# One write and one read per token tile for the hidden activations' way through DRAM, and logits of two partition halves issued in turn, in a one-core encoder layer

## The chip, the core and the metric

The kernel runs on one core of one Trainium2 chip. A core has five engines with a queue of their own: TensorE (PE, with PEld for the loads of its stationary operand), VectorE (DVE), ScalarE (ACT), GpSimd (POOL) and SyncE (SP). POOL and SP issue the transfers (DMAs) that move data between DRAM and the on-chip memory; a queue is worked off in order, so an instruction that waits holds all that stand behind it. The metric is the device time of one execution in microseconds (us), as a median of several runs.

## The reference

One layer of a streaming encoder on 256 tokens of width 2048, in float32. Four residual blocks follow each other, each closed by a layer norm of `ALPHA * x + block(x)`:

```
x <- LN(alpha*x + 0.5*SwiGLU_1(x))                             D_FF = 5632
x <- LN(alpha*x + W_o[g_A*(DiffAttn(x) W_A) + g_B*(DSA(x) W_B)])
x <- LN(alpha*x + MemCrossAttn(x, mem))
x <- LN(alpha*x + 0.5*SwiGLU_2(x))

_swiglu(x) = (silu(x @ w_gate) * (x @ w_up)) @ w_down

DiffAttn: 8 heads, each with two softmaxes over keys of width 64,  p0 - lam * p1
DSA index: score = sum over 16 heads of width 64 of  relu(iq_h . ik) * iw_h ; the 64 best keys are kept
```

The two softmaxes of a DiffAttn head, and two index heads at a time, lie in one tile of 128 partitions: the first 64 partitions hold one half, the other 64 the other. These are the logits that the change speaks of. The other part of the change sits in both SwiGLUs, between the product with `w_up` and the product with `w_down`.

## The kernel before, in words

Every matrix product is made of three passes: both operands are split into a high and a low part (`whi`, `wlo` for weights, `hh`, `hl` for the hidden activations), and `mm3` (L174 to L176) issues high*high, high*low and low*high. ACT makes the high part (L170), DVE the low part (L171). Weights come in units of 128x1024 numbers, 512 KB each, loaded by SP into `raw` (L183). A unit feeds 12 matmuls of 512 columns, six for token tile t = 0 (tokens 0 to 127) and then six for t = 1. `Feed` loads and splits units ahead of their use, up to 10 in the first SwiGLU and 8 in the second. The order on each engine is the order of the code: generators ("tasks") are stepped once after each unit (`tasks.tick()`), and what a step issues stands in the queues at that place.

A SwiGLU takes its 11 column blocks of 512 in groups of 4, 4 and 3 (`FFN_GROUPS`). For each block it computes gate and up, and then a task turns h = silu(gate)*up, which lies with tokens on the partitions, into `hh` and `hl` with features on the partitions. After a group, the product with `w_down` runs over the group's blocks; its first quarter reaches the last block's `hh` after six units. For the last block of a SwiGLU TensorE does the turn (`h_task`). For the other ten blocks of each of the two SwiGLUs, twenty in all, the turn goes through DRAM (`h_bounced`): DVE multiplies (L503), one unit later it transposes 32x32 blocks within partitions (L506, from `hnat` into the old `silu` tile), POOL writes each of the two token tiles to DRAM (`h_dram`) with four transfers of 64 KB (L509) and reads it back in another arrangement with one of 256 KB (L512, into `hnat`), and five units later (`BOUNCE`) ACT and DVE make `hh` and `hl` out of what came back. POOL's queue holds all eight writes of a block first, then both reads; a read waits until the four writes of its token tile have landed.

Logits of width 64 are computed by `logits` for DiffAttn and by the same three-pass code in `index_task`. One call makes one half: 128 queries by 128 keys, then 128 queries by 256 keys (`SEG`), three passes each, six matmuls on one half of the partitions, into one PSUM tile `tp` (four buffers). The call for the other half follows at once, so a pair is 12 matmuls; there are eight pairs for DiffAttn and eight for the index.

Of the kernel before, what the change touches and what calls it, by code (L numbers as in the profile page):

```python
# [9 lines left out]
F32 = mybir.dt.float32  # L10
F32R = mybir.dt.float32r
AF = mybir.ActivationFunctionType
ALU = mybir.AluOpType
# [3 lines left out]
P = 128  # L17
# [4 lines left out]
NCOL = 512  # L22
# [11 lines left out]
SEG = ((0, 128), (128, 384))  # L34
# [116 lines left out]
def tile_encoder_layer(ctx, tc, a, out):  # L151
    nc = tc.nc
# [8 lines left out]
    dram = ctx.enter_context(tc.tile_pool(name="dram", bufs=1, space=bass.MemoryType.DRAM))  # L161
# [4 lines left out]
    def tp():  # L166
        return ps_tp.tile([P, NCOL], F32, name="tp")

    def split(hi, lo, src):
        nc.scalar.copy(hi, src)  # L170
        nc.vector.tensor_tensor(lo, src, hi.bitcast(F32), ALU.subtract)  # L171

    def mm3(dst, lh, ll, rh, rl, start, stop):
        nc.tensor.matmul(dst, lh, rh, start=start, stop=False)  # L174
        nc.tensor.matmul(dst, lh, rl, start=False, stop=False)  # L175
        nc.tensor.matmul(dst, ll, rh, start=False, stop=stop)  # L176
# [163 lines left out]
    def transposed(src, hi, lo, width=NCOL):  # L340

        p = blocks_T(src, width)[:, :width]
        split(hi, lo, p.rearrange("p (b t) -> p b t", t=P) if len(hi.shape) == 3 else p)

    def new_xT():
        return base.tile([P, 2, KD, T], F32R, name="xT")

# [136 lines left out]
    def ffn(pre, pool, y, xT, sts, lead, end):  # L484

        for gi, (c0, c1) in enumerate(FFN_GROUPS):
            hT = []

            def h_task(s, u, hh, hl):
                h = [pool.tile([P, NCOL], F32, name="hnat", bufs=3) for _ in range(2)]  # L490
                for t in range(2):
                    nc.vector.scalar_tensor_tensor(h[t], s[t], 0.5, u[t], op0=ALU.mult, op1=ALU.mult)
                yield
                for t in range(2):
                    sl = slice(t * P, (t + 1) * P)
                    transposed(h[t], hh[:, :, sl], hl[:, :, sl])

            def h_bounced(s, u, hh, hl):

                h = [pool.tile([P, NCOL], F32, name="hnat", bufs=3) for _ in range(2)]  # L500
                via = dram.tile([P, 2, 4, P], F32, name="h_dram", bufs=4)
                for t in range(2):
                    nc.vector.scalar_tensor_tensor(h[t], s[t], 0.5, u[t], op0=ALU.mult, op1=ALU.mult)  # L503
                yield
                for t in range(2):
                    nc.vector.transpose(s[t].rearrange("p (g b i) -> p g b i", b=4, i=32),  # L506
                                        h[t].rearrange("p (b g i) -> p g b i", b=4, i=32))
                    for q in range(4):
                        nc.gpsimd.dma_start(via[:, t, q].rearrange("(g i) c -> i g c", i=32),  # L509
                                            s[t][32 * q:32 * q + 32].rearrange("i (g c) -> i g c", g=4))  # L510
                for t in range(2):
                    nc.gpsimd.dma_start(h[t].rearrange("p (q c) -> p q c", q=4), via[:, t])  # L512
                for _ in range(BOUNCE):
                    yield
                for t in range(2):
                    sl = slice(t * P, (t + 1) * P)
                    split(hh[:, :, sl].rearrange("p b (q j) -> p b q j", j=32),
                          hl[:, :, sl].rearrange("p b (q j) -> p b q j", j=32),
                          h[t].rearrange("p (q b j) -> p b q j", b=4, j=32))

            for c in range(c0, c1):
                g = product(x_lhs(xT), pre + "_w_gate", c, dense(KD), lead=lead if c == 0 else 0)
                s = [pool.tile([P, NCOL], F32, name="silu", bufs=2) for _ in range(2)]
                for t in range(2):
                    nc.scalar.activation(s[t], g[t], AF.Silu)
                u = product(x_lhs(xT), pre + "_w_up", c, dense(KD))
                hh = pool.tile([P, 4, T], F32R, name="hh", bufs=4)
                hl = pool.tile([P, 4, T], F32R, name="hl", bufs=4)
                tasks.spawn((h_task if c == DFF // NCOL - 1 else h_bounced)(s, u, hh, hl))
                hT.append((hh, hl))  # L530

            def h_lhs(k, t):
                hh, hl = hT[k // 4]
                sl = slice(t * P, (t + 1) * P)
                return hh[:, k % 4, sl], hl[:, k % 4, sl]

            final = gi == len(FFN_GROUPS) - 1
            for n in range(4):
                kts = down_kts(c0, c1)
                if final and n == 3:  # L540
                    def after(t, d):
                        add_chunk(y, t, 3, d, 1.0, sts)
                        end(t)
                    product(h_lhs, pre + "_w_down", n, kts, trail=SKEW, after=after)
                else:
                    d = product(h_lhs, pre + "_w_down", n, kts)
                    for t in range(2):
                        add_chunk(y, t, n, d[t], 1.0 if gi else ALPHA, sts if final else None)
# [44 lines left out]
    with tc.tile_pool(name="att", bufs=1) as att:  # L593
# [34 lines left out]
        distm = att.tile([P, 384], F32, name="distm")  # L628
# [6 lines left out]
        score = att.tile([P, 384], F32, name="score")  # L635
# [17 lines left out]
        def logits(q, k, rowsl, blk):  # L653
            p = tp()
            for t, (s0, s1) in enumerate(SEG):
                ts_ = slice(t * P, (t + 1) * P)
                mm3(p[:, s0:s1], q[rowsl, 0, blk, ts_], q[rowsl, 1, blk, ts_],
                    k[rowsl, 0, blk, :s1 - s0], k[rowsl, 1, blk, :s1 - s0], True, True)
            return p

        def softmax_exp(dist, slope, p):

            e = att.tile([P, 384], F32, name="e", bufs=4)
            nc.vector.scalar_tensor_tensor(e, dist, -slope, p[:, :384], op0=ALU.mult, op1=ALU.add)
            nm = stat.tile([P, 2], F32, name="nm")
            sm = stat.tile([P, 2], F32, name="sm")
            for t, (s0, s1) in enumerate(SEG):
                nc.vector.tensor_reduce(nm[:, t:t + 1], e[:, s0:s1], AX.X, ALU.max, negate=True)  # L668
                nc.scalar.activation(e[:, s0:s1], e[:, s0:s1], AF.Exp, bias=nm[:, t:t + 1],  # L669
                                     accum_out=sm[:, t:t + 1])  # L670
            return e, sm
# [7 lines left out]

        def diff_head(q, k, v, b, g, r):  # L680
            slope = 2.0 ** -(4 * g + b + 1)
            es = []
            for c in range(2):
                es.append(softmax_exp(distm, slope, logits(q, k, slice(c * 64, c * 64 + 64), b)))
            yield
            (e0, s0), (e1, s1) = es
            r0 = stat.tile([P, 2], F32, name="r0")
# [4 lines left out]
            for t, (a0, a1) in enumerate(SEG):  # L692
                nc.scalar.mul(e1[:, a0:a1], e1[:, a0:a1], r1[:, t:t + 1])
                nc.vector.scalar_tensor_tensor(e0[:, a0:a1], e0[:, a0:a1], r0[:, t:t + 1], e1[:, a0:a1],
                                               op0=ALU.mult, op1=ALU.subtract)
# [48 lines left out]
        p = w_in(2)  # L744
# [42 lines left out]
        def index_task():  # L787
            while not (tik.done and tq1.done and d1.done):
                yield
            yield  # L790
            for h in range(16):
                iq, b, half = (iq0, iq1)[h // 8], h % 8 // 2, h % 2
                rowsl = slice(half * 64, half * 64 + 64)
                pl = tp()
                for t, (s0, s1) in enumerate(SEG):
                    ts_ = slice(t * P, (t + 1) * P)
                    mm3(pl[:, s0:s1], iq[rowsl, 0, b, ts_], iq[rowsl, 1, b, ts_],
                        ikT[rowsl, 0, :s1 - s0], ikT[rowsl, 1, :s1 - s0], True, True)
                r = att.tile([P, 384], F32, name="relu", bufs=2)
                nc.scalar.activation(r, pl[:, :384], AF.Relu)  # L800
                for t, (s0, s1) in enumerate(SEG):
                    nc.vector.scalar_tensor_tensor(score[:, s0:s1], r[:, s0:s1], iw[:, t, h:h + 1],
                                                   score[:, s0:s1], op0=ALU.mult, op1=ALU.add)
                if h % 2:
                    yield
            for i in range(TOPK // 8):
                for t, (s0, s1) in enumerate(SEG):
                    m8 = stat.tile([P, 8], F32, name="m8")
                    nc.vector.max(m8, score[:, s0:s1])
                    nc.vector.match_replace(score[:, s0:s1], m8, score[:, s0:s1], NEG)  # L810
                yield
            nc.vector.tensor_scalar(dists, score, -2e38, BIG, op0=ALU.is_gt, op1=ALU.mult)
            nc.vector.tensor_tensor(dists, dists, distm, ALU.add)
# [343 lines left out]
```

## Time and profile before

| what | value |
|---|---|
| median of 3 runs | 2259.43 us (2257.69 to 2259.87) |
| the profiled execution: its time, its span | 2260.71 us, 2258.9 us |
| PE, PEld busy | 2237.8 us (99%), 1850.0 us (82%) |
| DVE, ACT, POOL busy | 1308.0 us (58%), 1035.9 us (46%), 131.5 us (6%) |
| DMA: mean over the span | 203 GB/s; the weights' queue 62.2% of the 16 DMA engines' time, POOL's queue 3.4% |
| PE clock granted | over 0.9 in all forty slices |

The span is the stretch from the first to the last instruction that the profiler saw; the run's time is 1.8 us longer. Matmuls are pipelined, and the ends that the profile gives them are modelled, so that a row's duration is longer than the step to the next row: in the products a 128x512 matmul starts every 0.23 us and is shown as 0.39 us. For TensorE it is the starts that tell the cost. "From issue to landing" of a transfer counts from the start of its issue on the queue.

### The profile page before, as it was taken

The numbers are of one execution on the slowest core, as the hardware profiler recorded it, in microseconds if no ns is written. First come the engines' busy times: TensorE is split into PE (matmuls) and PEld (weight loads), VectorE is DVE, ScalarE is ACT, GpSimd is POOL, SyncE is SP. The second block draws the span as 40 slices with busy tenths as digits, with TensorE's granted clock in tenths as the row PEclk, the third lists the DMA queues.
The fourth block names the chain that finished last, engine by engine and source line by source line (L and its number), as shares of the span: only waits on it lengthen the run. The fifth ranks groups of instructions, "written<-read, shape, count | busy, mean of one in ns | idle before, by whom it ended". The sixth has DMA issues, their size and how long they took to land.

```text
span 2258.9 us, 27277 instructions
## 1 busy us (share of the span) xinstructions
PE 2237.8 (99%) x10248; PEld 1850.0 (82%) x10248; DVE 1308.0 (58%) x1498; ACT 1035.9 (46%) x1317; POOL 131.5 (6%) x236
## 2 busy tenths in 40 slices
PE   9999999999999999999999999999999999999997
PEld 7888888888888888888888888878888888888886
DVE  6555555554556666685655556777555455554554
ACT  5443344444443555655544444655444344434442
POOL 0100000100000000000000000000000001100100
PEclk9999999999999999999999999999999999999999
DMA  8877677766665655445567667557776666766762
GB/s 272 315 236 212 190 210 215 213 207 195 212 209 168 209 159 165 151 147 170 183 193 207 202 224 263 174 168 227 221 251 207 194 213 212 230 192 191 221 198 91
DMA packets 128916, 458.26 MB, mean 203 GB/s; under 512 B 16704, under 2 KB 16832, under 8 KB 127632
## 3 DMA queue, kind: packets, MB, share of 16 engines
q1 hardware_dynamic: 119520, 431.02, 62.2%
q0 software_dynamic: 9264, 25.51, 3.4%
q8 instruction: 80, 1.31, 0.2%
q14 instruction: 52, 0.43, 0.1%
HBM read 441.78 MB, written 14.68 MB: 202 GB/s over the span
## 4 chain that ended last, share of the span: by engine, by line
PE 94%; DMA 2%; issue 1%; DVE 1%; ACT 1%; POOL 0%; POOLq 0%; SPq 0%; DVEq 0%; ACTq 0%
PE acc L174 30%; PE acc L176 30%; PE acc L175 30%; PE tp L337 2%; DMA hnat<-h_dram 1%; DMA h_dram<-silu 1%; PE tp L174 1%; PE tp L175 1%; PE tp L176 0%; DMA raw<-in_ffn_w_gate 0%; ACT whi L170 0%; DVE wlo L171 0%; POOL h_dram L509 0%; DVE y L479 0%; ACT me L1010 0%
## 5 line engine op out<-in xcount | busy, mean ns | idle before, releaser
L171 DVE TENSOR_TENSOR wlo<-raw,whi 128x1024 fp32r<-128x1024 f32 (+1 forms) x787 | 958.3, 1222 | 811.3 <-ACT whi L170 808.7
L170 ACT CAST whi<-raw 128x1024 fp32r<-128x1024 f32 (+1 forms) x787 | 824.1, 1051 | 932.5 <-PE acc L176 874.2
L174 PE MATMUL acc<-whi,xT 128*128 128x512 f32 x2176 | 853.8, 392 | 1.7 <-ACT whi L170 1.7
L176 PE MATMUL acc<-whi,xT 128*128 128x512 f32 x2176 | 848.3, 390 | 0.0
L175 PE MATMUL acc<-wlo,xT 128*128 128x512 f32 x2176 | 848.2, 390 | 0.0
L174 PEld LDWEIGHTS acc<-whi,xT 128*128 128x128 f32 x2176 | 409.2, 188 | 87.1 <-ACT whi L170 3.3
L176 PEld LDWEIGHTS acc<-whi,xT 128*128 128x128 f32 x2176 | 409.0, 188 | 86.0
L175 PEld LDWEIGHTS acc<-wlo,xT 128*128 128x128 f32 x2176 | 409.4, 188 | 84.4 <-DVE wlo L171 0.9
L174 PE MATMUL acc<-whi,hh 128*128 128x512 f32 x704 | 274.9, 390 | 2.3 <-ACT hh L170 2.3
L176 PE MATMUL acc<-whi,hl 128*128 128x512 f32 x704 | 274.4, 390 | 0.0
L175 PE MATMUL acc<-wlo,hh 128*128 128x512 f32 x704 | 274.0, 389 | 0.0
L174 PEld LDWEIGHTS acc<-whi,hh 128*128 128x128 f32 x704 | 132.1, 188 | 30.9 <-ACT hh L170 4.0
L176 PEld LDWEIGHTS acc<-whi,hl 128*128 128x128 f32 x704 | 132.1, 188 | 29.1 <-DVE hl L171 1.7
L175 PEld LDWEIGHTS acc<-wlo,hh 128*128 128x128 f32 x704 | 132.2, 188 | 27.3
L509 POOL DMA_DIRECT2D h_dram<-silu x160 | 87.2, 553 | 1077.0 <-DVE silu L506 1027.2
L174 PE MATMUL acc<-whi,ring 128*128 128x512 f32 x144 | 56.7, 394 | 0.0
L176 PE MATMUL acc<-whi,ring 128*128 128x512 f32 x144 | 56.1, 390 | 0.0
L175 PE MATMUL acc<-wlo,ring 128*128 128x512 f32 x144 | 56.1, 389 | 0.0
L479 DVE SCALAR_TENSOR_TENSOR y<-y,acc 128x512 f32<-128x512 f32 x64 | 42.2, 679 | 17.3 <-PE acc L176 17.3
L669 ACT ACTIVATE e<-e,nm 128x128 f32<-128x128 f32 (+1 forms) x48 | 21.5, 448 | 45.7 <-DVE nm L668 44.8
L170 ACT CAST hh<-hnat 128x512 fp32r<-128x512 f32 x40 | 24.8, 621 | 37.7 <-DMA hnat<-h_dram 34.8
L171 DVE TENSOR_TENSOR hl<-hnat,hh 128x512 fp32r<-128x512 f32 x40 | 27.4, 691 | 25.2 <-ACT hh L170 25.2
(200 smaller groups left out, 1136.6 us busy)
## 6 DMA issues: line engine op xcount, KB each, us to landing
raw<-in_ffn_w_up SPq DMA_DIRECT2D x176, 512.0 KB, 4.4
raw<-in_ffn_w_down SPq DMA_DIRECT2D x176, 512.0 KB, 4.2
raw<-in_ffn_w_gate SPq DMA_DIRECT2D x175, 512.0 KB, 4.3
raw<-in_w_in SPq DMA_DIRECT2D x88, 512.0 KB, 3.6
raw<-in_w_gate SPq DMA_DIRECT2D x64, 512.0 KB, 4.1
raw<-in_w_mix_out SPq DMA_DIRECT2D x32, 512.0 KB, 4.4
h_dram<-silu POOLq DMA_DIRECT2D x160, 64.0 KB, 4.4
hnat<-h_dram POOLq DMA_DIRECT2D x40, 256.0 KB, 5.3
```

Source lines behind the costliest of these rows:

```text
L170: nc.scalar.copy(hi, src)
L171: nc.vector.tensor_tensor(lo, src, hi.bitcast(F32), ALU.subtract)
L174: nc.tensor.matmul(dst, lh, rh, start=start, stop=False)
L175: nc.tensor.matmul(dst, lh, rl, start=False, stop=False)
L176: nc.tensor.matmul(dst, ll, rh, start=False, stop=stop)
L337: nc.tensor.transpose(p[:, b * P:(b + 1) * P], src[:, b * P:(b + 1) * P], ident)
L479: nc.vector.scalar_tensor_tensor(c, c, scale, d, op0=ALU.mult, op1=ALU.add)
L509: nc.gpsimd.dma_start(via[:, t, q].rearrange("(g i) c -> i g c", i=32), s[t][32 * q:32 * q + 32].rearrange("i (g c) -> i g c", g=4))
L669: nc.scalar.activation(e[:, s0:s1], e[:, s0:s1], AF.Exp, bias=nm[:, t:t + 1], accum_out=sm[:, t:t + 1])
```

## The change

Two things are changed. First, in `h_bounced`, DVE transposes with another order of features in its input (`turn`: feature b*128 + i*4 + g instead of b*128 + g*32 + i), and a token tile is written by one transfer of 256 KB with rows of 2 KB and read back by one of 256 KB whose pieces are 512 bytes (`to_places`; before, the writes had pieces of 512 bytes and the read had rows of 2 KB). Both transfers of a token tile are issued before those of the other. The features end in the same places. Second, `twin_logits` computes both halves of a pair in one loop that goes to the other half after each matmul, into two PSUM tiles.

```diff
+    def turn(dst, src):
+        nc.vector.transpose(dst.rearrange("p (g b i) -> p b g i", b=4, i=32),
+                            src.rearrange("p (b i g) -> p b g i", b=4, i=32))
+
+    def to_places(dst, src):
+        via = dram.tile([P, NCOL], F32, name="via", bufs=6)
+        nc.gpsimd.dma_start(via, src)
+        nc.gpsimd.dma_start(dst.rearrange("p (q c) -> p q c", q=4),
+                            via.rearrange("(q i) (g c) -> (i g) q c", q=4, g=4))
...
             def h_bounced(s, u, hh, hl):
...
-                via = dram.tile([P, 2, 4, P], F32, name="h_dram", bufs=4)
...
                 for t in range(2):
-                    nc.vector.transpose(s[t].rearrange("p (g b i) -> p g b i", b=4, i=32),
-                                        h[t].rearrange("p (b g i) -> p g b i", b=4, i=32))
-                    for q in range(4):
-                        nc.gpsimd.dma_start(via[:, t, q].rearrange("(g i) c -> i g c", i=32),
-                                            s[t][32 * q:32 * q + 32].rearrange("i (g c) -> i g c", g=4))
-                for t in range(2):
-                    nc.gpsimd.dma_start(h[t].rearrange("p (q c) -> p q c", q=4), via[:, t])
+                    turn(s[t], h[t])
+                    to_places(h[t], s[t])
...
+        def twin_logits(q, blk, key):
+            p = [tp(), tp()]
+            for t, (s0, s1) in enumerate(SEG):
+                ts_ = slice(t * P, (t + 1) * P)
+                for i, (a, b) in enumerate(((0, 0), (0, 1), (1, 0))):
+                    for half in range(2):
+                        rowsl = slice(half * 64, half * 64 + 64)
+                        nc.tensor.matmul(p[half][:, s0:s1], q[rowsl, a, blk, ts_], key(rowsl, b, slice(s1 - s0)),
+                                         start=i == 0, stop=i == 2)
+            return p
...
-            es = []
-            for c in range(2):
-                es.append(softmax_exp(distm, slope, logits(q, k, slice(c * 64, c * 64 + 64), b)))
+            es = [softmax_exp(distm, slope, p) for p in twin_logits(q, b, lambda r, h, c: k[r, h, b, c])]
...
-            for h in range(16):
...
+            for h in range(0, 16, 2):
+                pls = twin_logits((iq0, iq1)[h // 8], h % 8 // 2, lambda r, i, c: ikT[r, i, c])
+                for half, pl in enumerate(pls):
...
```

On POOL, the first block of the first SwiGLU before (`silu_300` and `silu_301` are the two token tiles, `hnat_458` and `hnat_459` where they come back to; the waits on DMASW are waits for transfers of POOL's own to land):

```order
L509 DMA h_dram_460<-silu_300 32x4x128 [waits DVE_49,Activation_49]
L509 DMA h_dram_460<-silu_300 32x4x128 x3
L509 DMA h_dram_460<-silu_301 32x4x128 [waits DVE_49,Activation_49]
L509 DMA h_dram_460<-silu_301 32x4x128
L509 DMA h_dram_460<-silu_301 32x4x128 [waits DMASW0_49]
L509 DMA h_dram_460<-silu_301 32x4x128 [waits DMASW1_49]
L512 DMA hnat_458<-h_dram_460 128x512 [waits DMASW4_49,DMASW5_49,DMASW3_49,DMASW2_49]
L512 DMA hnat_459<-h_dram_460 128x512 [waits DMASW6_49,DMASW7_49,DMASW1_49,DMASW0_49]
```

The same place now, with the transfer ahead of it (of the constant `lnT`):

```order
L324 DMA lnT_80<-in_lnT 128x128
L354 DMA via_483<-silu_300 128x512 [waits DVE_49,Activation_49]
L355 DMA hnat_458<-via_483 128x4x128 [waits DMASW2_49]
L354 DMA via_487<-silu_301 128x512 [waits DVE_49,Activation_49]
L355 DMA hnat_459<-via_487 128x4x128 [waits DMASW4_49]
```

Ten rows became four, and the second token tile's write now stands behind the first token tile's read, which waits for the first write to land. On PE, the logits of the first DiffAttn pair before (`tp_5953` is the first half, `tp_5968` the second):

```order
L174 MATMUL tp_5953<-ring_5762,ring_5578 128x128
L175 MATMUL tp_5953<-ring_5762,ring_5578 128x128
L176 MATMUL tp_5953<-ring_5762,ring_5578 128x128
L174 MATMUL tp_5953<-ring_5762,ring_5578 128x256
L175 MATMUL tp_5953<-ring_5762,ring_5578 128x256
L176 MATMUL tp_5953<-ring_5762,ring_5578 128x256
L174 MATMUL tp_5968<-ring_5762,ring_5578 128x128
L175 MATMUL tp_5968<-ring_5762,ring_5578 128x128
L176 MATMUL tp_5968<-ring_5762,ring_5578 128x128
L174 MATMUL tp_5968<-ring_5762,ring_5578 128x256
L175 MATMUL tp_5968<-ring_5762,ring_5578 128x256
L176 MATMUL tp_5968<-ring_5762,ring_5578 128x256
```

The same place now (the two halves are `tp_5903` and `tp_5904`):

```order
L681 MATMUL tp_5903<-ring_5712,ring_5528 128x128
L681 MATMUL tp_5904<-ring_5712,ring_5528 128x128
L681 MATMUL tp_5903<-ring_5712,ring_5528 128x128
L681 MATMUL tp_5904<-ring_5712,ring_5528 128x128
L681 MATMUL tp_5903<-ring_5712,ring_5528 128x128
L681 MATMUL tp_5904<-ring_5712,ring_5528 128x128
L681 MATMUL tp_5903<-ring_5712,ring_5528 128x256
L681 MATMUL tp_5904<-ring_5712,ring_5528 128x256
L681 MATMUL tp_5903<-ring_5712,ring_5528 128x256
L681 MATMUL tp_5904<-ring_5712,ring_5528 128x256
L681 MATMUL tp_5903<-ring_5712,ring_5528 128x256
L681 MATMUL tp_5904<-ring_5712,ring_5528 128x256
```

The twelve matmuls are the same; the halves take turns. On DVE, ACT and SP the instructions stand in the order in which they stood before.

## Rows read from the trace of the kernel before

**Rows 1.** The page's first part: busy time and share of each engine.
```profile
PE 2237.8 (99%) x10248; PEld 1850.0 (82%) x10248; DVE 1308.0 (58%) x1498; ACT 1035.9 (46%) x1317; POOL 131.5 (6%) x236
```

**Rows 2.** The page's chain that ended last: shares by engine.
```profile
PE 94%; DMA 2%; issue 1%; DVE 1%; ACT 1%; POOL 0%; POOLq 0%; SPq 0%; DVEq 0%; ACTq 0%
```

**Rows 3.** Waits of PE, for hh: us in total, times, longest.
```profile
PE acc L174 <- ACT hh L170: 2.3, 4, 0.6
```

**Rows 4.** Waits of ACT, for PE: us in total, times, longest.
```profile
ACT whi L170 <- PE acc L176: 874.2, 536, 9.8
```

**Rows 5.** Timeline of weight loads in the first logit pair: start us, us, instruction.
```profile
805.08 0.18 PEld L174 LDWEIGHTS tp<-ring 64*128 64x128 f32 x1 [0.35 <-issue]
805.19 0.19 PEld L175 LDWEIGHTS tp<-ring 64*128 64x128 f32 x1
...
805.37 0.23 PEld L174 LDWEIGHTS tp<-ring 64*128 64x128 f32 x2
...
805.69 0.19 PEld L174 LDWEIGHTS tp<-ring 64*128 64x128 f32 x1
...
805.93 0.18 PEld L176 LDWEIGHTS tp<-ring 64*128 64x128 f32 x1
806.25 0.19 PEld L174 LDWEIGHTS acc<-whi,xT 128*128 128x128 f32 x1
```

**Rows 6.** The same timeline, a narrower stretch: the second of the merged two.
```profile
805.41 0.19 PEld L174 LDWEIGHTS tp<-ring 64*128 64x128 f32 x1
```

**Rows 7.** Timeline of matmuls around that pair.
```profile
804.76 0.39 PE L176 MATMUL acc<-whi,xT 128*128 128x512 f32 x1
...
806.25 0.50 PE L174 MATMUL acc<-whi,xT 128*128 128x512 f32 x1
806.59 0.39 PE L175 MATMUL acc<-wlo,xT 128*128 128x512 f32 x1
```

**Rows 8.** The chain at the first group's end: start us, us, what.
```profile
187.84 1.35 POOL h_dram L509 x3
...
189.49 4.77 DMA h_dram<-silu
...
194.33 0.51 issue
194.85 5.60 DMA hnat<-h_dram
```

**Rows 9.** Timeline of POOL there: the second token tile's read.
```profile
196.24 0.55 POOL L512 DMA_DIRECT2D hnat<-h_dram  x1 [0.84 <-DMA h_dram<-silu]
```

**Rows 10.** Timeline of ACT there: both casts of what came back.
```profile
200.53 0.62 ACT L170 CAST hh<-hnat 128x512 fp32r<-128x512 f32 x1 [1.54 <-DMA hnat<-h_dram]
201.65 0.62 ACT L170 CAST hh<-hnat 128x512 fp32r<-128x512 f32 x1 [0.50 <-DMA hnat<-h_dram]
```

**Rows 11.** Timeline of DVE there: the low part after a weight unit's.
```profile
199.02 1.23 DVE L171 TENSOR_TENSOR wlo<-raw,whi 128x1024 fp32r<-128x1024 f32 x1 [1.50 <-ACT whi L170]
201.18 0.69 DVE L171 TENSOR_TENSOR hl<-hnat,hh 128x512 fp32r<-128x512 f32 x1 [0.93 <-ACT hh L170]
```

**Rows 12.** Timeline of matmuls there: the last before the wait, the first and fourth behind.
```profile
200.23 0.39 PE L176 MATMUL acc<-whi,hl 128*128 128x512 f32 x1
201.20 0.50 PE L174 MATMUL acc<-whi,hh 128*128 128x512 f32 x1 [0.58 <-ACT hh L170]
...
202.26 0.40 PE L174 MATMUL acc<-whi,hh 128*128 128x512 f32 x1
```

**Rows 13.** The first 64 KB write of that block alone: issue, and time to landing.
```profile
L509 POOL DMA_DIRECT2D h_dram<-silu x1: 567/567/567, 187.8 to 187.8; - x1
...
DMA to landing us min/median/max: 3.4/3.4/3.4
```

**Rows 14.** The forty reads of L512, to landing.
```profile
DMA to landing us min/median/max: 3.7/5.3/6.3
```

**Rows 15.** DMA issues: writes of 256 KB from a 128x512 tile elsewhere; KB, median us to landing.
```profile
x_dram<-y POOLq DMA_DIRECT2D x8, 256.0 KB, 2.3
```

**Rows 16.** Those eight writes, to landing.
```profile
DMA to landing us min/median/max: 2.3/2.3/4.8
```

**Rows 17.** Costliest groups of DVE: the transposes.
```profile
L506 DVE STREAM_TRANSPOSE silu<-hnat 128x512 f32<-128x512 f32 x40 | 26.0, 687 | 0.0
```

More of the change, by code (lines that the diff above doesn't have):

```diff
@@ L343, in transposed, with in_order, groups @@
         split(hi, lo, p.rearrange("p (b t) -> p b t", t=P) if len(hi.shape) == 3 else p)
+    def turn(dst, src):
[6 more added lines that the diff above has]
+                            via.rearrange("(q i) (g c) -> (i g) q c", q=4, g=4))
+    def in_order(x):
+        return x.rearrange("p (q b j) -> p b q j", b=4, j=32)
+    def groups(x):
+        return x.rearrange("p b (q j) -> p b q j", j=32)
     def new_xT():
@@ L516, in h_bounced @@
                     sl = slice(t * P, (t + 1) * P)
-                    split(hh[:, :, sl].rearrange("p b (q j) -> p b q j", j=32),
-                          hl[:, :, sl].rearrange("p b (q j) -> p b q j", j=32),
-                          h[t].rearrange("p (q b j) -> p b q j", b=4, j=32))
+                    split(groups(hh[:, :, sl]), groups(hl[:, :, sl]), in_order(h[t]))
             for c in range(c0, c1):
@@ L790, in index_task @@
             yield
-            for h in range(16):
[L792 to L805, printed above, removed]
+            for h in range(0, 16, 2):
+                pls = twin_logits((iq0, iq1)[h // 8], h % 8 // 2, lambda r, i, c: ikT[r, i, c])
+                for half, pl in enumerate(pls):
+                    r = att.tile([P, 384], F32, name="relu", bufs=2)
+                    nc.scalar.activation(r, pl[:, :384], AF.Relu)
+                    for t, (s0, s1) in enumerate(SEG):
+                        nc.vector.scalar_tensor_tensor(score[:, s0:s1], r[:, s0:s1], iw[:, t, h + half:h + half + 1],
+                                                       score[:, s0:s1], op0=ALU.mult, op1=ALU.add)
+                yield
             for i in range(TOPK // 8):
```

## The prediction

> **What bounds the kernel now.** I read the page's busy times first, then its chain, then the waits of TensorE (PE), then the two stretches that the change touches. PE is busy for 99% of the span [rows 1], and 94% of the chain is PE [rows 2]. So a microsecond taken off PE's own steps is a microsecond off the end, and one on another engine counts only where PE waits for it. The splitting of weights is no limit: ACT spends 874 us waiting for PE to release a unit's place [rows 4], so PE always has units ready, some eight of them at 12 x 0.23 us each. Of the two SwiGLUs only one thing makes PE wait: four times it waits for `hh` [rows 3], at the end of the first and second group of each SwiGLU, where the last block of the group has come back from DRAM too late. The view counts 2.3 us, but the timeline shows more. The last matmul before the wait starts at 200.23; the next would start at 200.46, the fourth behind it at 201.14, and that fourth starts at 202.26 [rows 12]: 1.12 us are lost, 0.74 waiting for the high part and 0.38 after it, largely for the low part that DVE makes behind ACT. Four such places cost 4.5 us. At the other sixteen blocks a late `hh` makes only ACT and DVE wait, and the units in stock cover that.
>
> **Logits in turn: a gain of 3.7 us.** A pair of halves is 12 matmuls. Between the last product matmul before it, 804.76, and the second after it, 806.59 [rows 7], lie 1.83 us; two ordinary steps would take 0.46, so a pair costs 1.37 us, 16 pairs 22 us. How the time is spent is seen in the loads of the stationary operand. Within one half a load follows the one before by 0.11 us (805.08 to 805.19) [rows 5]. But where the second half has begun (805.37) while the first half's second segment (805.41 [rows 6]) is still running, loads of the two halves come 0.04 to 0.07 us apart, each half keeping its own 0.11 us. So the two halves of the partitions already work side by side, for the middle third: first three matmuls alone, then three and three together, then three alone, from 805.08 to 805.93 [rows 5], 0.85 us. Issued in turn, the two sides run together all the way: 11 steps of 0.055 us, and a little more for the 256-column ones, 0.62 us. Saved: 0.23 us a pair, 3.7 us in 16 pairs, all on PE. Upper bound: if both halves start together at each step, five steps of 0.11 to 0.12, 0.28 saved, 4.5 us. Lower bound: the pattern brings nothing (0), or a switch of halves after every matmul costs the full 0.11 us, 11 x 0.11 = 1.21 instead of 0.85, a loss of 5.8 us; the middle of the pair, where halves already alternate, speaks against that, and I don't count on it. The wait of the first half's softmax moves not at all or to earlier, since its last matmul now comes one step before the end of a shorter pair; ACT and DVE have room there.
>
> **The way through DRAM: a loss of 4 us at the four places, nothing elsewhere.** What is removed: POOL's issue of six of the eight writes of a block (8 x 0.55 us become 2 x 0.55). What is added: a wait in POOL's queue. Before, all eight writes were issued in a row and both reads followed; now the second token tile's write stands behind the first tile's read, and that read waits until the first write has landed. Two landings of writes stand in series where there was one.
>
> The old way at the first place: the first write is issued at 187.84, the last of the first tile lands at 194.33, its read is issued 0.52 us later and lands 5.60 us after that [rows 8]; the second tile's read is issued at 196.24 [rows 9] and has landed when ACT casts at 201.65 [rows 10], 13.8 us after the first issue. The new way, with W0 and W1 for the writes, R for the second read, 0.52 from a landing to the next issue and 0.56 for an issue of a read: W0 + 0.52 + 0.56 + W1 + 0.52 + R = W0 + W1 + R + 1.60.
>
> W has no row of its own kind. Elsewhere eight writes of the same size and shape took 2.3 us [rows 15], the slowest 4.8 [rows 16]; here, among the weights' transfers, the first 64 KB alone took 3.4 [rows 13], and a whole tile has four times that. I take W0 = 3.8, and W1 = 4.3, since it queues behind the first read. R: forty reads took 3.7 to 6.3, median 5.3 [rows 14]; the new read has pieces of 512 bytes instead of 2 KB, and I take 5.3. Sum: 15.0 us, so the second tile is there at 202.84 instead of 201.6, the first at about 197.5 instead of 200.45.
>
> Then at each of the four places: the first tile's high part is cast in time; its low part stands behind a weight unit's (199.02 + 1.23 [rows 11]), is ready at 200.97 and costs 0.1. The second tile is first needed six matmuls after 200.46, at 201.93 with that 0.1. Its high part is ready 0.70 us after landing (0.62 for the cast [rows 10] and the handing over), 203.54: 1.61 us of waiting, and 0.37 behind it as now. That makes 2.08 us instead of 1.12, a loss of 0.96, four times 3.8 us. From about 14.0 us on (landing at 201.9) the new way loses, with 4 us for each microsecond more.
>
> Bounds: with 2.3 + 2.3 + 3.7 + 1.6 = 9.9 us nothing is late but that 0.1, a gain of 4.1; with 4.8 + 4.8 + 6.3 + 1.6 = 17.5 the landing is at 205.34, 4.58 us a place, a loss of 13.8. DVE's transpose reads every fourth number now; at 687 ns for 512 columns [rows 17] it takes a number per column, and I leave it at that. Were it twice as long, the first write would start 0.69 later: 2.8 us in the four places, and the other 27 us hidden, as DVE is busy for 58% [rows 1].
>
> The Trainium skill, "DMA: Bandwidth & Descriptors", section "Anatomy of one DMA — SWDGE (gpsimd) path", fits a transfer as about 2.0 us plus its bytes at 436 GB/s. An estimate by it: 2.6 us for 256 KB, either way, so 9.4 us in all and the gain of 4.1 above. The quiet writes of [rows 15] agree; the 64 KB of [rows 13] took 3.4 where the fit gives 2.2, so among the weights it falls short.
>
> **Sum.** -3.7 + 3.8 = +0.1 us. The profiled execution took 2260.71 us, of which 2258.9 are the span, and lies 1.3 above the median of 2259.43; I set the difference against the median: 2259.5 us.
>
> **Rivals.**
> Quick writes (faster): the old writes were slow because of their 512-byte pieces, and rows of 2 KB land as in the quiet stretch, 2.3 to 3.4 us. For: [rows 15]. Against: 3.4 us for a mere 64 KB here [rows 13]. With 2.6 + 3.0 + 5.0 + 1.6 = 12.2 us the landing is at 200.0, before the need, and each place gains about 1.0: 4 us, with the logits 7.7, 2251.7 us. Decided by a landing before 13.8 us: from there on the sum is more than 4.5 us faster.
> Slow scattered reads (slower): a read of 512 pieces instead of 128 costs POOL or the transfer engines more. All POOL transfers in this trace have about 128 pieces and 0.55 us of issue, so whether issue goes by pieces isn't seen; if it did, each read would be issued in 2.2 us instead of 0.56, 1.65 later for the second write and 1.65 for the second read. 15.0 + 3.3 = 18.3 us, 5.4 us a place, 17 us lost: 2272.7 us. At 16.1 us, with slower reads and writes alone, the sum passes +4.5: 2264.
> The Trainium skill, "DMA: Bandwidth & Descriptors", in that same section, calls the making of descriptors small and says that many can be made before it shows; that speaks against the higher of these two prices, and no row here shows it either way.
> No gain from the logits: 2263.2 us, if the reordering that PE now does by itself leaves nothing to win.
>
> **How the numbers follow.** What a measurement of this kernel can tell from no change is about 0.2%, 4.5 us: 2254.9 to 2263.9. The forecast, a landing 13.8 to 16.1 us after the first issue with the logits' gain, 0.43, or without it, 0.03: within. Quick writes or a larger gain from the logits: 0.22, faster. Slow reads, serial writes over 16 us, a slower transpose: 0.32, slower. The likeliest alone spans 2255 to 2264; leaving out one in ten at each end, the range goes from the quick writes, 2252, to near the end of the slow ones, 2270.
>
> **What would show it.** In the changed kernel: loads of a pair 0.05 to 0.06 us apart from its first to its last, and 1.1 us for a pair instead of 1.37. On POOL: the second write issued a landing after the first, and the second read 9 to 11 us after the first write. On PE: the four waits for `hh` move from the first token tile's to the second's matmuls, about 2 us each. I am wrong if a write of 256 KB lands in under 3 us there (the waits vanish), if a read's issue on POOL takes far more than 0.56 us, or if the pair keeps its 0.85 us.

## The result: 0.6% slower, and the profile after

| | before | changed |
|---|---|---|
| median | 2258.59 us (6 runs) | 2272.18 us (6 runs, 2268.08 to 2276.19) |
| profiled execution: its time, its span | as in the table before | 2268.51 us, 2266.7 us |

The ratio is 1.0059, with a 95% interval of 1.0045 to 1.0073: slower by 13.6 us, and above the range of the prediction, which ended at 2270. The six runs of the changed kernel lie in two heaps, three near 2268.5 and three near 2275.7; the profiled execution belongs to the lower one, so it shows 9 to 10 us of the 13.6.

Busy times and the chain by engine, from the page of the changed kernel:

```profile
PE 2237.7 (99%) x10248; PEld 1848.3 (82%) x10248; DVE 1318.5 (58%) x1498; ACT 1029.0 (45%) x1317; POOL 74.0 (3%) x116
PE 93%; DMA 3%; issue 1%; DVE 1%; ACT 1%; POOL 0%; SPq 0%; POOLq 0%; ACTq 0%; DVEq 0%
```

PE's wait for `hh`, from its waits (us in total, times, longest):

```profile
PE acc L174 <- ACT hh L170: 10.3, 4, 4.6
```

POOL has 57.5 us less to do than in [rows 1], and the kernel is slower all the same. The wait of [rows 3] is still there at the same four places, but is 10.3 us instead of 2.3, and the longest is 4.6. The way of one block at the first place, from POOL's timeline (start us, us, instruction, idle before it and what ended it):

```profile
187.89 0.55 POOL L354 DMA_DIRECT2D via<-silu  x1 [30.86 <-ACT whi L170]
191.88 0.75 POOL L355 DMA_DIRECT2D hnat<-via  x1 [3.44 <-DVE wlo L171]
192.62 0.55 POOL L354 DMA_DIRECT2D via<-silu  x1
199.72 0.75 POOL L355 DMA_DIRECT2D hnat<-via  x1 [6.55 <-DMA via<-silu]
```

The wait before 191.88 is put down to DVE there; by its semaphore (under "The change") the read waits for the first write, which landed at 191.34. The chain of waits that ended last, in the same stretch:

```profile
187.89 3.45 DMA via<-silu
...
192.62 6.81 DMA via<-silu
199.43 0.28 issue
199.72 5.96 DMA hnat<-via
...
205.75 0.63 ACT hh L170
```

The first token tile's write needs 3.5 us, less than the four old writes; the second one's, of the same size and shape, 6.8. From the first issue to the second tile's landing it is 17.8 us (187.89 to 205.68), where it was at most 13.8 in [rows 8 to 10]. The first tile is in time now, but with its six matmuls done PE has nothing left to do. Matmuls there:

```profile
201.39 0.40 PE L176 MATMUL acc<-whi,hl 128*128 128x512 f32 x1
206.42 0.64 PE L174 MATMUL acc<-whi,hh 128*128 128x512 f32 x1 [4.63 <-ACT hh L170]
206.86 0.63 PE L175 MATMUL acc<-wlo,hh 128*128 128x512 f32 x1
207.29 0.65 PE L176 MATMUL acc<-whi,hl 128*128 128x512 f32 x1
...
209.45 0.63 PE L175 MATMUL acc<-wlo,hh 128*128 128x512 f32 x1
209.88 0.47 PE L176 MATMUL acc<-whi,hl 128*128 128x512 f32 x1
210.18 0.40 PE L174 MATMUL acc<-whi,hh 128*128 128x512 f32 x1
```

Two things are lost: a step of 5.03 us where 0.23 would do, and behind it eight steps of about 0.43 us instead of 0.23. The second is TensorE's clock. Windows of PE (length, busy time and count of each engine, granted clock, DMA share, GB/s) at the first, second and third place:

```profile
200.00:206.00 6.00, 1.79 (x8) 0.97 (x6) 0.54 (x1) 0.25 (x1) 0.47 (x1) 1.00 0.50 160
206.00:209.00 3.00, 2.58 (x6) 1.84 (x7) 1.92 (x2) 1.32 (x2) 0.00 (x0) 0.60 0.02 5
...
474.00:477.00 3.00, 3.00 (x10) 2.40 (x9) 1.91 (x2) 0.84 (x1) 0.00 (x0) 0.62 0.55 175
1724.00:1728.00 4.00, 4.00 (x19) 3.31 (x18) 2.83 (x4) 2.10 (x2) 0.00 (x0) 1.00 0.49 144
```

Behind the waits at the first two places the granted clock is 0.60 and 0.62, that is, for most of the stretch the lower of the two levels (1.2 instead of 2.4 GHz); at the third it stays at 1.00. Place by place, with the change against before taken from the starts of the same product matmuls in both traces:

| place | first issue to second tile's landing | step at the wait | slow steps | change |
|---|---|---|---|---|
| 1 | 17.8 us | 5.03 us | 8 | +5.5 us |
| 2 | 15.0 us | 2.27 us | 7 | +2.9 us |
| 3 | 14.8 us | 2.07 us | 0 | +1.2 us |
| 4 | 15.2 us | 2.50 us | 0 | +1.7 us |

Together +11.3 us. The logits give back 4.5 us, of which 0.6 is lost again. The first logit pair after, as matmuls:

```profile
812.90 0.39 PE L176 MATMUL acc<-whi,xT 128*128 128x512 f32 x1
813.22 0.96 PE L681 MATMUL tp<-ring 64*128 64x128 f32 x12
814.11 0.50 PE L174 MATMUL acc<-whi,xT 128*128 128x512 f32 x1
814.45 0.39 PE L175 MATMUL acc<-wlo,xT 128*128 128x512 f32 x1
```

From 812.90 to 814.45 it is 1.55 us, less two ordinary steps 1.09 us for a pair, against 1.37 in [rows 7]: 0.28 saved, sixteen times. Behind the fifteenth pair PE reaches its transposes 0.6 us earlier than before, but DVE writes what the last of them read no earlier: 5.9 us after the start of the fourteenth pair, in both kernels. So the gain of these two pairs is lost in a wait:

```profile
PE tp L337 <- DVE nat L844: 0.7, 1, 0.7
```

The kernel before has no such wait, and every run below that has the new logits has it. Net, the logits give 4.0 us. Another 2.0 us were lost around 1520.0, where PE waits for a layer norm in both kernels and, of these two executions, the clock fell in this one only; the start gained 0.3. That makes 11.3 - 4.5 + 0.6 + 2.0 - 0.3 = 9.1 us, by which the last product matmul starts later; the spans differ by 7.8, since what follows that matmul ended 1.3 us sooner in this execution.

### The profile page after: what moved, and what is told of

The parts are those of the page before. It is cut to its first block, busy times and chain, and to the rows that moved or that the text cites. A ratio compares the mean times of both kernels' runs of the same rounds, so it can differ in the third digit from the quotient of the medians.

```text
span 2266.7 us, 27045 instructions
## 1 busy us (share of the span) xinstructions
PE 2237.7 (99%) x10248; PEld 1848.3 (82%) x10248; DVE 1318.5 (58%) x1498; ACT 1029.0 (45%) x1317; POOL 74.0 (3%) x116
## 4 chain that ended last, share of the span: by engine, by line
PE 93%; DMA 3%; issue 1%; DVE 1%; ACT 1%; POOL 0%; SPq 0%; POOLq 0%; ACTq 0%; DVEq 0%
PE acc L174 30%; PE acc L176 30%; PE acc L175 30%; PE tp L337 2%; DMA via<-silu 1%; DMA hnat<-via 1%; PE tp L681 1%; DMA raw<-in_ffn_w_gate 1%; ACT whi L170 0%; DVE wlo L171 0%; PE tp L176 0%; PE tp L174 0%; PE tp L175 0%; DVE y L499 0%; ACT me L1026 0%
## 5 line engine op out<-in xcount | busy, mean ns | idle before, releaser
L174 PE MATMUL acc<-whi,hh 128*128 128x512 f32 x704 | 276.3, 392 | 10.3 <-ACT hh L170 10.3
L354 POOL DMA_DIRECT2D via<-silu x40 | 22.0, 550 | 1027.3 <-ACT whi L170 995.2
```

The source lines that it names most:

```text
L354: nc.gpsimd.dma_start(via, src)
```

## The experiments

All ran against the kernel before, in two groups, with medians of it of 2259.41 (the first four) and 2259.25 (the last four).

**The parts apart.** The first kernel is the one before with `twin_logits` alone:

```diff
...
-                es.append(softmax_exp(distm, slope, logits(q, k, slice(c * 64, c * 64 + 64), b)))
+            es = [softmax_exp(distm, slope, p) for p in twin_logits(q, b, lambda r, h, c: k[r, h, b, c])]
...
```

> Only the logits in turn; h goes through DRAM as before. The changed kernel's trace shows 0.28 us less per pair on TensorE, sixteen times. If TensorE's steps are all that counts there: 4.5 us under the kernel before, about 2254. If the loss of the changed kernel came from the logits in some hidden way (softmaxes later, PSUM tiles held longer): no gain, or slower than 2259.

Measured: 2255.25 us, ratio 0.9983 (0.9974 to 0.9992), 4.2 us faster. The gain of the logits stands by itself. The second is the changed kernel with the old logits:

```diff
...
-            es = [softmax_exp(distm, slope, p) for p in twin_logits(q, b, lambda r, h, c: k[r, h, b, c])]
...
+                es.append(softmax_exp(distm, slope, logits(q, k, slice(c * 64, c * 64 + 64), b)))
...
```

> Only the new way through DRAM; logits as before. If both parts add up: the changed kernel plus 4.5 us, about 2276 (2272 to 2281), a loss of 13 to 22 us against the kernel before. If the logits had part in the loss: less than that.

Measured: 2275.74 us, ratio 1.0072 (1.0059 to 1.0084), 16.3 us slower. The two parts add up to +12.2, near the whole change's 13.6. So all of the loss, and more, is the way through DRAM. In this trace the steps at the four waits are 1.64, 3.21, 4.03 and 4.72 us, and the clock fell behind the last three.

**Both writes ahead of both reads.** The changed kernel with nothing but the order of POOL's four transfers set back (`away` is the first half of `to_places`: it writes and returns `via`):

```diff
...
                 for t in range(2):
                     turn(s[t], h[t])
-                    to_places(h[t], s[t])
+                vias = [away(s[t]) for t in range(2)]
+                for t in range(2):
+                    to_places(h[t], vias[t])
...
```

> The changed kernel with one thing other: both token tiles' writes are issued before both reads. Theory of the order (the second write queues behind the first read, 6.6 us to land where the first took 3.5): the second tile is back some 12 us after the first write's issue instead of 17.8, the four waits on hh vanish, about 2250 us, 8 to 10 below the kernel before. Theory of the shape (reads of 512 pieces and the slower transpose cost the time, whatever the order): the second tile stays at 15 us or more, about 2262 to 2268.

Measured: 2250.86 us, ratio 0.996 (0.9948 to 0.9973): 8.5 us faster than before and 21 faster than the change. POOL's timeline at the first place, and the matmuls where PE waited:

```profile
188.22 0.56 POOL L354 DMA_DIRECT2D via<-silu  x1 [36.22 <-ACT whi L170]
189.21 0.56 POOL L354 DMA_DIRECT2D via<-silu  x1 [0.43 <-issue]
192.41 0.76 POOL L358 DMA_DIRECT2D hnat<-via  x1 [2.63 <-DMA via<-silu]
194.96 0.76 POOL L358 DMA_DIRECT2D hnat<-via  x1 [1.79 <-DMA via<-silu]
```

```profile
200.91 0.49 PE L176 MATMUL acc<-whi,hl 128*128 128x512 f32 x1
201.24 0.40 PE L174 MATMUL acc<-whi,hh 128*128 128x512 f32 x1
201.47 0.39 PE L175 MATMUL acc<-wlo,hh 128*128 128x512 f32 x1
```

The second read is issued 6.7 us after the first write, not 11.8. PE's wait for `hh` is gone from its waits altogether; the 1.1 us that each place cost before is down to 0.1. The second write, now behind a write, takes 4.9 us in the median of twenty blocks, not 6.2. The transfers, their pieces and the slower transposes are those of the change; the order alone decides.

**The old transfers in the new order.** The kernel before, only with each token tile's read right behind its own four writes:

```diff
                         nc.gpsimd.dma_start(via[:, t, q].rearrange("(g i) c -> i g c", i=32),
                                             s[t][32 * q:32 * q + 32].rearrange("i (g c) -> i g c", g=4))
-                for t in range(2):
                     nc.gpsimd.dma_start(h[t].rearrange("p (q c) -> p q c", q=4), via[:, t])
```

> The kernel before with one thing other: the first token tile's read is issued right behind its four writes, ahead of the second tile's four writes. Transfers, their pieces, the transpose and the logits are those of before. Theory of the order: the second tile is back at about 18 us instead of 13.8, and the kernel is 10 to 17 us slower than before, 2269 to 2276. Theory of the shape: the old pieces cost little, at most 3 us slower, 2259 to 2262.

Measured: 2281.42 us, ratio 1.0095 (1.0081 to 1.0109), 22 us slower; each of the four places costs 5.0 to 5.4 us more than before, and the clock fell at all four. POOL's timeline at the first one, and PE's waits:

```profile
188.44 2.17 POOL L509 DMA_DIRECT2D h_dram<-silu  x4 [27.42 <-DVE silu L506]
194.96 0.56 POOL L511 DMA_DIRECT2D hnat<-h_dram  x1 [4.35 <-DMA h_dram<-silu]
195.83 2.18 POOL L509 DMA_DIRECT2D h_dram<-silu  x4 [0.31 <-issue]
202.76 0.56 POOL L511 DMA_DIRECT2D hnat<-h_dram  x1 [4.75 <-DMA h_dram<-silu]
```

```profile
PE acc L174 <- ACT hh L170: 14.8, 8, 3.5
```

The same order hurts the old form more, since both tiles now come late (eight waits, not four). It also gives the price of the two forms side by side: a tile's read could be issued 6.5 us after its first 64 KB write, and 4.0 us after the one write of 256 KB in the change. The new form of the transfers is better; its order is what costs.

**The transpose.** In the change DVE's transposes take longer than in [rows 17]. From the costliest groups (busy time, mean ns):

```profile
L349 DVE STREAM_TRANSPOSE silu<-hnat 128x512 f32<-128x512 f32 x40 | 41.5, 1077 | 0.0
```

Here the columns of the gate and up weights are laid out in the turned order beforehand, so that the transpose reads neighbouring numbers again; the transfers stay as in the change:

```diff
         nc.vector.transpose(dst.rearrange("p (g b i) -> p b g i", b=4, i=32),
-                            src.rearrange("p (b i g) -> p b g i", b=4, i=32))
+                            src.rearrange("p (b g i) -> p b g i", b=4, i=32))
```

> The changed kernel with one thing other: the columns of both SwiGLUs' gate and up weights lie in DRAM in the order that the turned features have, so that DVE's transpose reads neighbouring numbers again (as in the kernel before), and all else, the order on POOL too, is that of the changed kernel. If the transpose's step is what made it 1.08 us instead of 0.69: back to 0.69, the first write of a block 0.4 us earlier, 1.6 us in four places, about 2270 (2267 to 2272). If the transpose is a main cause of the loss: more than 5 us.

```profile
L349 DVE STREAM_TRANSPOSE silu<-hnat 128x512 f32<-128x512 f32 x40 | 26.0, 687 | 0.0
```

Measured: 2266.27 us, ratio 1.0028 (1.0019 to 1.0037), with 11 runs from 2261.18 to 2270.28. The transposes are back at 687 ns, and the kernel is 5.9 us under the change, more than the 0.39 us that each first transpose gives, four times. Where the rest comes from isn't shown. The trace is of the slowest of the eleven runs, 2270.28, which is slower than the profiled execution of the change; over its twenty blocks the median from first issue to second landing is 15.7 us instead of 17.1, with the second write at 5.2 instead of 6.2, but the first at 4.4 instead of 3.6, and the four places cost 14.8 us more than before in it, where they cost 11.3 in the change. The same edit on top of the writes-first order:

> Both: weights' columns laid out so that the transpose reads neighbours, and both writes ahead of both reads. With the writes first TensorE waited no more for hh, so a quicker transpose has nothing left to win: 2250 to 2251, the same as with the writes first alone. If the transpose held something up elsewhere on DVE: up to 2 us less.

Measured: 2250.45 us, ratio 0.9963 (0.995 to 0.9976), the same as without the edit. With the writes first the slow transposes are hidden; they matter only where the block comes late.

**The pieces of the read.** The changed kernel, whose reads take whole rows of 2 KB as the writes left them, so that the numbers land in other places than they belong:

```diff
-        nc.gpsimd.dma_start(dst.rearrange("p (q c) -> p q c", q=4),
-                            via.rearrange("(q i) (g c) -> (i g) q c", q=4, g=4))
+        nc.gpsimd.dma_start(dst, via)
```

> The changed kernel with reads of whole rows (128 pieces of 2 KB) in place of 512 pieces of 512 bytes; the order on POOL stays, one tile after the other. What is read back lies in the wrong places, so h is not the reference's; all else runs as in the changed kernel. If the pieces of the first read are what makes the second write take 6.6 us: it lands in about 4 to 4.5, the second tile is back at 15 us instead of 17.8, the kernel at 2258 to 2264. If it is any read ahead of it in the queue: 6 us or more remain, 2268 to 2273.

POOL's timeline at the first place:

```profile
188.38 0.54 POOL L354 DMA_DIRECT2D via<-silu  x1 [31.38 <-ACT whi L170]
192.00 0.54 POOL L355 DMA_DIRECT2D hnat<-via  x1 [3.08 <-DMA via<-silu]
192.53 0.54 POOL L354 DMA_DIRECT2D via<-silu  x1
200.33 0.54 POOL L355 DMA_DIRECT2D hnat<-via  x1 [7.26 <-DMA via<-silu]
```

Measured: 2269.35 us, ratio 1.0044 (1.003 to 1.0058). The issue of a read is down from 0.75 to 0.54 us, but the second write still takes over 7 us here and 6.7 in the median of twenty blocks, and 10.1 us of the 13.6 remain. So it isn't the 512-byte pieces of the read that hold up the write behind it; a read of whole rows does so too.

**The clock behind the waits.** The changed kernel with eight matmuls of 512 columns, on data that nobody uses, put in front of the second token tile's part of the unit that waits:

```diff
...
             half(0, i)
+            if fill is not None and i == nu - 2:
+                fill()
             half(1, i)
...
```

> The changed kernel with eight matmuls of 512 columns more at each of the four places, ahead of the second token tile's first matmul on the last block, into a PSUM tile that nobody reads: 1.8 us of work in a wait of 1.8 to 4.8 us. If the wait alone is the loss: unchanged, 2268 to 2276 in the same two heaps. If the clock that falls to half in the longer waits is part of it (matmuls at 0.43 us instead of 0.23 for some 2 to 4 us behind a wait): it falls less often, 2 to 6 us less, and the upper heap goes.

Measured: 2272.96 us, ratio 1.0053 (1.0039 to 1.0068), no different from the change, and still in two heaps. Matmuls at the first place, and the windows behind three of the waits:

```profile
202.54 1.98 PE L555 MATMUL tp<-xT 128*128 128x512 f32 x8
206.87 0.50 PE L174 MATMUL acc<-whi,hh 128*128 128x512 f32 x1 [2.35 <-ACT hh L170]
...
208.40 0.63 PE L176 MATMUL acc<-whi,hl 128*128 128x512 f32 x1
```

```profile
207.00:210.00 3.00, 3.00 (x9) 2.14 (x10) 1.76 (x2) 1.65 (x2) 0.00 (x0) 0.73 0.00 0
...
474.00:477.00 3.00, 3.00 (x8) 2.03 (x8) 1.60 (x2) 1.15 (x2) 0.00 (x0) 0.60 0.14 15
1724.00:1727.00 3.00, 2.81 (x11) 2.01 (x12) 1.92 (x2) 1.88 (x3) 0.00 (x0) 1.00 0.00 0
```

The fill fitted into the waits at no cost, but the clock fell behind three of the four all the same. By its time the run falls on the branch "the wait alone is the loss"; but since the slow matmuls stayed, it doesn't test that, and the clock's share is not isolated by it. What is known of it comes from the traces: 0.2 us a matmul, for eight and seven of them in the profiled execution of the change, 3 us, and for 27 in the kernel with the new way alone, 5.4 us.

## Why the prediction was wrong, step by step

**Right: the place and the mechanism.** PE waits at the same four places; the first token tile comes in time, the second too late, because its write stands behind the first tile's read. The rule that each microsecond beyond a landing 14.0 us after the first issue costs one at each place holds within 0.3 us, if the slow steps are added and the 0.36 us by which the first issue itself comes later (see the transpose): 17.8 - 14.0 + 1.6 + 0.4 = 5.8 at the first place (measured 5.5), and 2.8, 1.2 and 1.6 at the others (2.9, 1.2, 1.7).

**Right, with two errors that nearly cancel: the logits.** 3.7 us were forecast. PE's steps gave 4.5, the upper bound: the twelve loads start two at a time, from 813.22 to 813.79, with steps of 0.11 us between, as the bound supposed, and not one by one at 0.055 us as the sum did. But 0.6 us of it is lost again in the wait for `nat`, which the prediction did not see ("ACT and DVE have room there"). Net it is 4.0 us in the profiled execution, and 4.2 us by the run with the logits alone. The rival without this gain fell.

**Wrong: the second write, W1.** The sum took 4.3 us for it, half a microsecond more than for the first write, "since it queues behind the first read". Measured are 6.8 at the first place and 6.2 in the median of twenty blocks, against 3.6 for the first write (predicted 3.8). The failed step is that I let the write run beside the read. The read ahead of it at the first place was issued at 191.88 and landed 6.6 us later, at 198.45; the write behind it landed at 199.4. In the twenty blocks of this kernel, and in the twenty of each of the other four with this order of the new transfers, that is 100 of 100: the write landed 0.6 to 1.6 us after the read ahead of it, never before. With the old transfers in this order, each of the second tile's writes did the same in 20 of 20 blocks. So three transfers stand in series, W0 + R + R, where the sum had W0 + W1 + R with a short W1. With this kernel's medians, 3.6 for the first write, 5.9 for the first read, 0.9 from there to the second write's landing, 5.0 for the second read and 0.3 from a landing to the next issue, it is 3.6 + 0.3 + 5.9 + 0.9 + 0.3 + 5.0 = 16.0, by medians of the pieces, which needn't add up to the median of the totals, 17.1; the forecast was 15.0.

At places 2 to 4 of the profiled execution the total came out as forecast, 14.8 to 15.2, but by luck: the second write took 5.5, 4.7 and 4.9 us there, and the second read, 4.2 to 4.8, was quicker than the 5.3 of the sum. The four places cost 11.3 us, where 3.8 were forecast; of the 7.5 us more, about 2.8 are the late landing at the first place, 3.0 the slow matmuls at the first two, and 1.4 the later first issue. The last two are the terms below.

The Trainium skill, "DMA: Bandwidth & Descriptors", section "Queues, rings and completion order", says, of transfers that SP and ACT issue, that the mark of completion is an ordered write, which lands only after every earlier write of the same DMA engine, across its queues. POOL's transfers here behave as if it held for them too (100 of 100). The mark is not all of it: by the trace's records of single packets POOL's queue moved nothing from 191.0 to 194.8, so the second write, issued at 192.62, had moved nothing after 2.1 us, where the first write's packets began 1.3 us after its issue. Which of the packets from 194.8 on are the read's and which the write's, the records don't tell. The prediction priced the transfers one by one, and did not ask what one does to the next.

**Wrong: the transpose.** "I leave it at that", 687 ns, was 1077 ns: every fourth number is read more slowly. Its price was given, 2.8 us if it doubled, but the sum took nothing. Against the same matmuls on PE, a block's first issue comes 0.36 us later than before at each of the four places, 1.4 us together; the run that undid it brought the issue back to within 0.03 us, and gained 5.9. The rest of that gain is open. The Trainium skill, "Vector Engine (DVE) Microarchitecture Reference", section "5.2 Measured stream behaviour on trn2 (trn3 not measured)", gives, for an XOR of two sources, 1.73 instead of 1.05 ns per column when one source hops 4 KiB at every element. An estimate from that is 0.35 us more for 512 columns; 0.39 was measured here, for a transpose with hops of 16 bytes.

**Wrong by being left out: the clock.** Nothing in the sum stood for what comes behind a wait. Before, the step from one matmul to the next over a wait was 1.0 us, and the granted clock stayed at 1.00; of such steps of 1.9 to 5 us now, some are followed by 6 to 12 matmuls at the lower level, 1.2 to 2.4 us each. The length alone doesn't tell which: in the profiled execution of the change a step of 2.27 us was followed by it, and one of 2.50 was not. The shortest is in the run with the even transpose, a step of 1.92 us up to 469.31; PE's window behind it:

```profile
469.50:472.50 3.00, 3.00 (x10) 2.06 (x10) 1.71 (x2) 1.71 (x2) 0.00 (x0) 0.73 0.06 20
```

**The rivals.** The slow scattered reads gave 2272.7, nearly the time measured, but that is luck: a read's issue is 0.75 us, not 2.2, and with rows of 2 KB three quarters of the loss are left. What it did name, the serial order passing 16.1 us, is what happened at the first place (17.8) and in the median of the twenty blocks (17.1), but not at the other three places of the profiled execution. The quick writes were half right: 3.5 us among the weights' loads, where four old ones took 6.4; the order kept that from paying, and with the writes first it paid 4.2 us, beside the logits' 4.0.

**Open.** Which places make the two heaps of times, why a faster transpose gained more than its own 1.4 us, and why the clock falls behind one wait and not behind a like one.

## What to carry to other kernels

Where one queue carries several round trips, try all the writes ahead of all the reads: here a write put behind a read landed only after that read in every block, and a round trip that had been half hidden cost nearly its whole length again. Fewer and larger transfers, and a POOL with less to do, are worth nothing if their order makes the last piece later; ask of each reordering which piece is needed last, and follow that piece alone. When a wait of TensorE grows to some microseconds, allow for slow matmuls behind it, as here behind some waits and not behind others. And when TensorE gets quicker, look for the wait that this uncovers, as that for `nat` here.

## What the runs showed of the hardware

- A 256 KB write with rows of 2 KB landed in 3.6 us among the weights' loads, four of 64 KB with pieces of 512 bytes about 6 us after the first issue; behind a write of its own size it took 4.9, behind a read of 256 KB 6.2 (medians of twenty blocks), and then always landed after that read.
- Issuing a read of 512 pieces took POOL 0.75 us, one of 128 pieces 0.54: 0.2 us for four times the pieces.
- A transpose of 128x512 float32 took 1077 ns when reading every fourth number, and 687 when reading neighbours.
- Twelve matmuls of 64 rows, issued for the two halves of the partitions in turn, took 1.09 us instead of 1.37, with no loss for changing halves.
- TensorE's clock fell to its lower level behind waits that made a step as short as 1.9 us, for 6 to 12 matmuls at 0.43 us each, and in like places it didn't; filling the first part of such a wait with other matmuls didn't prevent it.
